# The indexer's keys and 176 of retention's value columns in natural form in the first product

## The chip, the cores and the metric

The kernel runs on one core of one Trainium2 chip. The time is the device time of one execution in microseconds; the time before is the median of three runs, 1668.37 us (1668.28 to 1669.16).

## The reference

One layer of a streaming encoder block on 512 tokens of 2048 channels, all in float32. The normalised input goes through one projection, whose output is cut into the operands of two mixers and two gates. What matters here:

```python
h = rmsnorm(x, norm_gain)
proj = h @ w_in
(aq, ak, av, az, iq, ik, iw, rq, rk, rv, rz, ga, gb) = jnp.split(proj, SPLIT_POINTS, axis=-1)
iq = iq.reshape(B, L, IDX_HEADS, IDX_DIM) * (IDX_DIM ** -0.5)   # 16 heads x 64
ik = plain_layernorm(ik)                                        # 64 columns, normalised per token
iw = iw * (IDX_HEADS ** -0.5)                                   # 16 columns
a_out = dsa_mixer(aq, ak, av, iq, ik, iw, positions, rel_bias) * jax.nn.silu(az)
...
rv = rv.reshape(B, L, R_HEADS, R_VAL_DIM)                       # 8 heads x 128 = 1024 columns
b_out = retention_mixer(rq, rk, rv, ret_gn_gain) * jax.nn.silu(rz)
merged = jax.nn.sigmoid(ga) * (a_out @ w_a_out) + jax.nn.sigmoid(gb) * (b_out @ w_b_out)
r = x + merged @ w_o
return r + (p_i @ w_ple) * jax.nn.sigmoid(r @ w_ple_gate)
```

The index scores are `relu(iq . ik)` weighted with `iw` and summed over the 16 heads; each query keeps its 128 best keys by them.

## The kernel before

**Numbers and products.** A float32 product is made of three matmuls of split operands: `high*high`, `high*low`, `low*high`. The input's parts are `hparts[k]` (names `hh` and `hl`, 128 channels by 512 tokens, for the 16 tiles k of the 2048 channels). A weight arrives by DMA as `wraw`; ScalarE (ACT) converts it to the high part `wh` (L153), VectorE (DVE) subtracts to get the low part `wl` (L158). Such a piece of weight is a unit. There are three buffers each of `wh` and `wl`, so `split_to` works at most two units ahead of the one in use, and `load_to` issues the DMAs five units further ahead from SP's queue, into seven buffers (`RAW_BUFS`).

**Two forms.** In the transposed form the weight is the stationary operand and 384 or 512 tokens move through; the result has channels on partitions. In the natural form 128 tokens of `hh` or `hl` are stationary and weight columns move; the result has tokens on partitions, and there are four token tiles.

**The stages that matter here.** (1) The first product, `gemms` over `u_ik`: the 80 columns `ik` and `iw` in the transposed form (`ps_ikw`, all 512 tokens), and the first 384 columns of `iq` as three blocks (`ps_iq`, 384 tokens), for k = 0 to 15. The weight `w_ik` holds 464 columns. Beside it the input is loaded, split (`x_split`) and squared for the norm (`rms_acc`). (2) The other five blocks of `iq`, meanwhile the norm's sum, and `f_keys1`, `f_keys2`, `f_keys3`: the keys are turned to natural form by four transposes on PE (`ps_kn`), normalised, doubled and turned back. (3) `values`: retention's 1024 value columns in natural form, two blocks of 512 (`ps_vn`, L763 to L765), 16 k by four token tiles by three products each. The blocks are scaled by the token's norm on ACT (L772) and stored to `rd`, from which each head of retention loads its 128 columns much later. Meanwhile PE also makes the index scores (`ps_is`), ACT and DVE sum them (`relu`, `isc`), and the tiles of h are prepared for what follows (`x_steps`: `xn_norm`, and the sums and splits in `combos`, names `ha`, `hs`, `t`). (4) `values_pair`: the attention values, in seven products of units of two k (`ps_v...`, L963 to L965).

**The order of the work.** It is written out by hand; nothing is reordered. PE's loops call `step()` after each group of matmuls (three, in the stages above). A step runs what `later` put on that step, then takes one entry of the queue `todo`; an entry `None` is an empty place. If the entry was empty or `todo` is, and the step's number is a multiple of `state["rate"]`, it takes one entry of the background queue `bg`. So the other engines' instructions are issued in program order at a place that is counted in PE's steps; when they run depends on their engine's own queue and on what they wait for. `todo` holds first the splits of the input (66 entries for the 64 steps of the first product), then the norm, the keys and the index scores; `bg` holds the 8 rounds of `x_steps` (six entries each), some empty entries, the rounds of the top-k and the position bias. The rate is 2 during `values` and 5 during `values_pair`.

Of the kernel before, what the change touches and what calls it, by code (L numbers as in the profile page):

```python
# [9 lines left out]
F32 = mybir.dt.float32  # L10
# [7 lines left out]
L = 512  # L18
# [14 lines left out]
PI_CLAMP = 3.1415925  # L33


def block_kernel(tc, xT, pT, posb, posq, w_in, w_v, w_ik, w_a, w_b, w_o, w_ple, w_gate,
                 w_gt, w_pt, fgb, tab, gains, cst, dec, out, out_a, out_b):
    nc = tc.nc
    pe, dve, act, pool, sp = nc.tensor, nc.vector, nc.scalar, nc.gpsimd, nc.sync
# [1 line left out]
    with contextlib.ExitStack() as ctx:  # L41
# [10 lines left out]
        def U(name, dt=F32):  # L52
            return up.tile([128, L], dt, name=name, tag="u")
# [4 lines left out]
        def P(name):  # L58
            return pp.tile([128, L], F32, name=name, tag="p")
# [122 lines left out]
        def step():  # L182
            tick[0] += 1
            while soon and soon[0][0] <= tick[0]:
                heapq.heappop(soon)[2]()
            f = todo.popleft() if todo else None
            if f is not None:
                f()
            elif bg and (tick[0] % state["rate"] == 0 or state["owed"]):
                state["owed"] = state["hold"]  # L190
                if not state["hold"]:
                    bg.popleft()()
# [145 lines left out]


        K8 = (8, 8)  # L340
        col = lambda g, m: w_in[g + m]
        AQ, AK, AZ, IQ, RQ, RK, RZ, GA, GB = 0, 8, 16, 24, 32, 40, 48, 56, 72
        u_ik = block(w_ik, (1,) * 4 + (2,) * 6, 464)
        u_iq = [None] * 3 + [block(col(IQ, m), K8) for m in range(3, 8)]
        u_rv = [block(w_v[i], (2,) * 8, 512) for i in range(2)]
        u_av = block_wide_pair(w_v[2], w_v[3])
        u_r, u_g = [], []
        for h in range(NH):
            u_r.append(block_pair(col(RQ, h), col(RK, h)))
# [19 lines left out]
        ng, fg, gn = g_sb[:, 0:16], g_sb[:, 16:32], g_sb[:, 32:40]  # L369
        xs = []  # L370
        for k in range(KT):
            if k in (1, 2, 3, 4, 5, 7, 9, 11, 13, 15):
                load_to(state["raw"] + 1)
# [67 lines left out]
        x_split(0)  # L441
        split_to(1)
        step()
        x_split(1)
        split_to(2)
        step()
        sp.dma_start(cs, cst)
        sp.dma_start(pos_i, posb)
# [3 lines left out]
        for k in range(2, KT):  # L452
            todo.append(lambda k=k: x_split(k))
            if k == 2:
                todo.extend([None] * 3)
            else:
                todo.extend([None, None if k % 2 else lambda k=k: rms_acc(xs[k // 2 - 2], k // 2 - 2)] + [None] * (k < 6))
        for k in range(6, KT):
            todo.extend([lambda k=k: rms_acc(xs[k], k), None])

        ps_ikw, *ps_iqs = gemms([(u_ik, slice(0, 80), hparts, ALL, "ps_ikw")]
                                 + [(u_ik, slice(a, a + 128), hparts, slice(128, L), "ps_iq") for a in (80, 208, 336)], 2)

        def iq_split(ps):
            ta = U("ta", F32R)
# [16 lines left out]
        def f_rnat():  # L482
# [4 lines left out]
            dve.tensor_scalar(r2w, r2w, 2.0 ** -5, None, op0=OP.mult)  # L487
            R["r2w"] = r2w


        wq = cp.tile([128, NT, 16], F32, name="wq")

        def f_keys1():
            ps = P("ps_kn")
            for t in range(NT):
                pe.transpose(ps[:, 128 * t:128 * t + 80], kraw[:80, tok(t)], ident[:80, :80])
            kn = U("kn")
            kst = S("kst", 24)
            kmv = S("kmv", 8)
            for t in range(NT):  # L500
                c = slice(128 * t, 128 * t + 64)
                dve.tensor_scalar(kn[:, c], ps[:, c], R["nat"][:, t:t + 1], None, op0=OP.mult)
                dve.tensor_scalar(wq[:, t, :], ps[:, 128 * t + 64:128 * t + 80], R["r2w"][:, t:t + 1], None,
                                  op0=OP.mult)
# [95 lines left out]
            R["ct"], R["st"] = ct, st  # L600

        N3 = [None] * 3
        todo.extend(N3 * 2 + [f_sum] + N3 * 3 + [f_rnat] + N3 * 3 + [f_bcast, None, f_keys1] + N3 * 3 + [f_keys2] + N3 * 2 + [f_keys3] + N3 * 2)
        later(80, f_pos)
        later(88, f_table1)
        later(92, f_table2)
# [48 lines left out]
            return load + [lambda: xn_norm(k)] + [lambda i=i: h_step(k, i) for i in range(X_STEPS)]  # L655

        for m in range(3):
            index_tile(m, ix[m])
# [93 lines left out]
        def values(ids, name, each=lambda s: None):  # L752

            pss = [P("ps_vn") for _ in range(NT)]
            seq = ksteps(ids)
            for s, (i, k) in enumerate(seq):
                if k == 0:
                    split_to(i + AHEAD)
                    load_to(i + AHEAD + LOADS)
                h, l = loaded[i]  # L760
                a, b = hparts[s]
                for t in range(NT):
                    pe.matmul(pss[t], a[:, tok(t)], h[:, k], start=(s == 0), stop=False)  # L763
                    pe.matmul(pss[t], a[:, tok(t)], l[:, k], start=False, stop=False)  # L764
                    pe.matmul(pss[t], b[:, tok(t)], h[:, k], start=False, stop=(s == KT - 1))  # L765
                    step()
                each(s)
            return pss

        def normal(ps, name, t, dt=F32):  # L770
            v = U(name, dt)
            act.activation(v, ps, AF.Copy, scale=R["nat"][:, t:t + 1])  # L772
            return v
# [4 lines left out]
        rd = dp.tile([2, NT, 128, L], F32, name="rd")  # L778

        def retention(h):  # L780

            hc = slice(128 * (h % 4), 128 * (h % 4) + 128)
# [3 lines left out]
            later(32, lambda: sp.dma_start(rv.rearrange("p (t c) -> p t c", t=NT),  # L786
                                           rd[h // 4, :, :, hc].rearrange("t p c -> p t c")))
            ct, st = R["ct"], R["st"]
            E = {}

# [105 lines left out]

        for i in range(2):
            for t, ps in enumerate(values(u_rv[i], "rv", x_load if i else lambda s: None)):
                later(3 * t, lambda i=i, t=t, ps=ps: act.dma_start(rd[i, t], normal(ps, "rv", t)))
        state["rate"] = BG_RATES[1]  # L900


# [471 lines left out]
        todo.extend([None] * 4 + [a_rms, None, a_bc])  # L1374
        todo.extend([lambda m=m: (a_out(m), a_out(m + 1)) for m in range(0, 16, 2)])

        pg, pw = P("ps_tg"), [P("ps_tw") for _ in range(2)]
# [41 lines left out]
            (sp, act, sp)[q].dma_start(out_b[:, L * q:L * q + L], o)  # L1419


MF = 12
U_BUFS = 69
BIG_BUFS = 5
# [20 lines left out]
def _layout(x, p, positions, w_in, norm_gain, w_a_out, w_b_out, w_o, ret_gn_gain,  # L1445
# [8 lines left out]
    def chans(v):  # L1454
# [11 lines left out]
    o["w_v"] = np.concatenate([tiles(w[:, a:a + 1024], 512) for a in (7248, 2048)])  # L1466
    o["w_ik"] = np.ascontiguousarray(
        np.concatenate([w[:, 5120:5200], w[:, 4096:4480]], axis=1).reshape(KT, 128, 464).transpose(1, 0, 2))
# [64 lines left out]
```

## Time and profile before

| | |
|---|---|
| median of three runs | 1668.37 us |
| the profiled execution | 1668.73 us, span 1666.9 us |
| PE (matmuls), PEld (weight loads) busy | 99%, 87% of the span |
| DVE, ACT, POOL busy | 75%, 56%, 15% |
| first product | 5.01 to 42.34 us |
| the other `iq` blocks | 42.34 to about 93.5 us |
| `values`, two blocks | about 93.5 to 191.07 us, the second from 147.55 |
| HBM read, written | 300.21 MB, 41.42 MB |

All times below are microseconds from the start of the span. Matmuls are pipelined: the duration of one is longer than the distance to the start of the next, and that distance is what a further matmul costs. "Idle before" an instruction is idle time of its engine, with what ended it in brackets.

### The profile page before, as it was taken

Reading aid. Unit: us, or ns where it says so; the run is one execution under the profiler, and the core shown is the slowest. Engines: PE = TensorE matmul, PEld = TensorE weight load, DVE = VectorE, ACT = ScalarE, POOL = GpSimd, SP = SyncE. Lnnn points to the kernel's source line nnn. Section 1 sums busy time; section 2 is a strip of 40 time slices with the busy share of each in tenths; the row PEclk is TensorE's granted clock in tenths of the full one; section 3 lists DMA queues with packets and bytes.
Section 4 is the critical chain, followed back from the end, with each engine's and each line's share of the span. In section 5 each row is a group of like instructions: output and inputs, shape, how many; then the busy total and the mean of one; then the engine's idle time right before and its main releaser. Section 6 shows DMA issues by size and latency. Waiting matters only on the chain.

```text
span 1666.9 us, 24622 instructions
## 1 busy us (share of the span) xinstructions
PE 1658.6 (99%) x9174; PEld 1443.8 (87%) x9174; DVE 1252.0 (75%) x1907; ACT 936.8 (56%) x1428; POOL 246.4 (15%) x262
## 2 busy tenths in 40 slices
PE   9999999999999999999999999999999999999998
PEld 8988888888888888888888888888888888888897
DVE  7788889888888888777766676777668887864454
ACT  6556545555555555777776665566633544463342
POOL 2000112111111111111431112100000111112221
PEclk9999999999999999999999999999999999999999
DMA  7327989788788788788898888997466788733222
GB/s 304 114 89 238 320 255 263 202 209 219 192 207 215 192 205 218 204 204 240 238 252 222 220 220 214 268 371 271 154 219 190 186 226 218 205 114 102 83 69 101
DMA packets 121559, 343.25 MB, mean 206 GB/s; under 512 B 13728, under 2 KB 21664, under 8 KB 121440
## 3 DMA queue, kind: packets, MB, share of 16 engines
q1 hardware_dynamic: 84640, 229.71, 40.0%
q0 software_dynamic: 25712, 92.03, 29.5%
q10 hardware_dynamic: 11088, 19.95, 3.3%
q8 instruction: 72, 1.18, 0.3%
q14 instruction: 47, 0.39, 0.1%
HBM read 300.21 MB, written 41.42 MB: 205 GB/s over the span
## 4 chain that ended last, share of the span: by engine, by line
PE 96%; DVE 2%; ACT 1%; issue 0%; DMA 0%; DVEq 0%; SPq 0%; ACTq 0%
PE ps_p L286 24%; PE ps_v L286 16%; PE ps_q L286 8%; PE ps_r L286 8%; PE ps_w L217 3%; PE ps_w L218 3%; PE ps_w L216 3%; PE ps_pg L218 3%; PE ps_pg L217 3%; PE ps_pg L216 3%; PE ps_vn L763 2%; PE ps_vn L765 2%; PE ps_vn L764 2%; PE ps_iq L216 1%; PE ps_iq L217 1%; PE ps_iq L218 1%
## 5 line engine op out<-in xcount | busy, mean ns | idle before, releaser
L158 DVE TENSOR_TENSOR wl<-wraw,wh 128x1024 fp32r<-128x1024 f32 (+3 forms) x460 | 557.2, 1225 | 177.4 <-ACT wh L153 169.4
L153 ACT ACTIVATE wh<-wraw 128x1024 fp32r<-128x1024 f32 (+3 forms) x460 | 474.0, 1040 | 229.6 <-DVE wraw L160 115.4
L119 POOL DMA_DIRECT2D wraw<-w_in x120 | 106.5, 956 | 580.2 <-DVE wl L158 358.6
L286 PE MATMUL ps_p<-hs,wh 128*128 128x512 f32 x640 | 161.1, 393 | 0.0
L249 ACT ACTIVATE e<-ps_p 128x512 f32<-128x512 f32 x144 | 85.9, 596 | 111.7 <-PE ps_p L286 110.0
L286 PEld LDWEIGHTS ps_p<-hs,wh 128*128 128x128 f32 x640 | 114.9, 189 | 20.7 <-issue 0.3
L286 PE MATMUL ps_p<-hs,wl 128*128 128x256 f32 x640 | 92.3, 284 | 0.0
L286 PEld LDWEIGHTS ps_p<-hs,wl 128*128 128x128 f32 x640 | 83.2, 192 | 0.5 <-issue 0.4
L286 PE MATMUL ps_q<-ha,wh 128*128 128x512 f32 x320 | 80.7, 393 | 0.0
L286 PE MATMUL ps_v<-ha,wh 128*128 128x512 f32 x320 | 80.1, 392 | 0.0
L695 ACT ACTIVATE mk<-relf,thr 128x512 f16<-128x512 f32 (+3 forms) x128 | 68.3, 555 | 20.1 <-DVE go L986 13.6
L286 PE MATMUL ps_p<-ha,wh 128*128 128x512 f32 x320 | 79.3, 389 | 0.0
L286 PE MATMUL ps_r<-hs,wh 128*128 128x512 f32 x320 | 79.1, 389 | 0.0
L286 PE MATMUL ps_v<-hs,wh 128*128 128x512 f32 x320 | 79.0, 389 | 0.0
L218 PE MATMUL ps_pg<-rh,wl 128*128 128x512 f32 x192 | 74.8, 390 | 0.0
L217 PE MATMUL ps_pg<-rl,wh 128*128 128x512 f32 x192 | 74.7, 389 | 0.0
L216 PE MATMUL ps_pg<-rh,wh 128*128 128x512 f32 x192 | 74.7, 389 | 0.0
L119 POOL DMA_DIRECT2D wraw<-w_o x24 | 20.9, 931 | 348.8 <-DVE wl L158 316.8
L986 DVE TENSOR_TENSOR go<-e_t 128x256 f32<-128x256 f32 x160 | 68.0, 425 | 5.7
L286 PEld LDWEIGHTS ps_p<-ha,wh 128*128 128x128 f32 x320 | 60.0, 188 | 12.7 <-issue 0.3
L286 PEld LDWEIGHTS ps_r<-hs,wh 128*128 128x128 f32 x320 | 60.1, 188 | 12.5
L286 PEld LDWEIGHTS ps_v<-hs,wh 128*128 128x128 f32 x320 | 60.1, 188 | 12.5
(414 smaller groups left out, 3713.2 us busy)
## 6 DMA issues: line engine op xcount, KB each, us to landing
wraw<-w_in SPq DMA_DIRECT2D x170, 512.0 KB, 5.3
wraw<-w_in POOLq DMA_DIRECT2D x120, 512.0 KB, 8.3
wraw<-w_v SPq DMA_DIRECT2D x32, 512.0 KB, 4.7
wraw<-w_o SPq DMA_DIRECT2D x32, 512.0 KB, 4.8
wraw<-w_o POOLq DMA_DIRECT2D x24, 512.0 KB, 6.4
wraw<-w_gate SPq DMA_DIRECT2D x24, 512.0 KB, 3.8
wraw<-w_b SPq DMA_DIRECT2D x16, 512.0 KB, 5.9
wraw<-w_a SPq DMA_DIRECT2D x16, 512.0 KB, 3.8
```

The lines of the kernel that those rows point to most:

```text
L119: pool.dma_start(out=view(raw_tiles[r], nk, cols), in_=src[:, k0:k0 + nk, :], accum_op=OP.add)
L153: act.activation(h, raw, AF.Copy)
L158: dve.tensor_sub(l, raw, h.bitcast(F32))
L216: pe.matmul(o, h[:, k, w], a, start=(s == order[0]), stop=False)
L217: pe.matmul(o, h[:, k, w], b, start=False, stop=False)
L218: pe.matmul(o, l[:, k, w], a, start=False, stop=(s == order[-1]))
L249: act.activation(E[n], src, AF.Copy)
L286: pe.matmul(o[:, c], w[:, k], X[PRODUCTS[n]][k][:, c], start=(n < 4 and first and k == 0), stop=(ended[n] == 16), skip_group_check=True)
L695: act.activation(bias_e[b][:, ln * i:ln * i + ln], relf[:, :ln], AF.Sign, bias=thr[:, q:q + 1])
L763: pe.matmul(pss[t], a[:, tok(t)], h[:, k], start=(s == 0), stop=False)
L764: pe.matmul(pss[t], a[:, tok(t)], l[:, k], start=False, stop=False)
L986: dve.tensor_add(o[:, q], c0, c1)
```

## The change

The weight `w_ik` now has 640 columns a k: the 80 of `ik` and `iw`, 176 value columns of retention, and the 384 of `iq`. The first product makes the first 256 of them (`N0`) in natural form, four token tiles in four banks, and the 384 of `iq` as before, so each k has 12 + 9 matmuls and seven steps. Each k is a unit of its own; the first k is loaded and split in two pieces. The other 848 value columns are made by `values` in two blocks of 424. The keys come out in natural form, so the four transposes in `f_keys1` go; the 176 value columns are copied to SBUF with the keys (`raw_n`), and scaled and stored to `rd` by four entries that stand in places of `todo` that were empty. `rd` has one row of 1024 columns a token. The entries of `todo` during the first product are spread over its 112 steps. `PHASE` shifts the count of steps that the background goes by, and `FILL` gives the background a fourth empty entry.

```diff
-            elif bg and (tick[0] % state["rate"] == 0 or state["owed"]):
+            elif bg and ((tick[0] + PHASE) % state["rate"] == 0 or state["owed"]):
...
-        u_ik = block(w_ik, (1,) * 4 + (2,) * 6, 464)
+        u_ik = block(w_ik[:, :, 0:N0], (1,), N0) + block(w_ik[:, :, N0:640], (1,), 384)
+        u_ik += [len(units) + i for i in range(KT - 1)]
+        units.extend((raw(w_ik, k, 1, 640), None, 1, 640) for k in range(1, KT))
...
-        u_rv = [block(w_v[i], (2,) * 8, 512) for i in range(2)]
-        u_av = block_wide_pair(w_v[2], w_v[3])
+        u_rv = [block(w_r[i], (2,) * 8, RV[2] - RV[1]) for i in range(2)]
+        u_av = block_wide_pair(w_v[0], w_v[1])
...
             if k == 2:
-                todo.extend([None] * 3)
+                todo.extend([None] * 6)
             else:
-                todo.extend([None, None if k % 2 else lambda k=k: rms_acc(xs[k // 2 - 2], k // 2 - 2)] + [None] * (k < 6))
+                todo.extend([None, None if k % 2 else lambda k=k: rms_acc(xs[k // 2 - 2], k // 2 - 2)]
+                            + [None] * (4 if k < 6 else 1))
...
-        ps_ikw, *ps_iqs = gemms([(u_ik, slice(0, 80), hparts, ALL, "ps_ikw")]
-                                 + [(u_ik, slice(a, a + 128), hparts, slice(128, L), "ps_iq") for a in (80, 208, 336)], 2)
+        ps_n, ps_iqs = [P("ps_vn") for _ in range(NT)], [P("ps_iq") for _ in range(3)]
+        for s, i in enumerate(u_ik[1:]):
+            split_to(i + 2)
+            load_to(i + AHEAD + LOADS)
+            (h, l), (a, b) = loaded[i if s else 0], hparts[s]
+            first, last = s == 0, s == KT - 1
+            for t in range(NT):
+                o = ps_n[t][:, 0:N0]
+                pe.matmul(o, a[:, tok(t)], h[:, 0, 0:N0], start=first, stop=False)
+                pe.matmul(o, b[:, tok(t)], h[:, 0, 0:N0], start=False, stop=False)
+                pe.matmul(o, a[:, tok(t)], l[:, 0, 0:N0], start=False, stop=last)
+                step()
+            h, l = loaded[i]
+            for j in range(3):
...
-        kraw = U("kraw")
-        act.activation(kraw[:80, :], ps_ikw[:80, :], AF.Copy)
-        ix = [iq_split(ps) for ps in ps_iqs[0:2]] + [[]]
-        later(12, lambda i=ix[2]: i.extend(iq_split(ps_iqs[2])))
+        raw_n = [U("raw_n").rearrange("p (a c) -> p a c", a=2) for _ in range(2)]
+        ix3 = [[] for _ in range(3)]
+        for t in range(NT):
+            act.activation(raw_n[t // 2][:, t % 2, 0:N0], ps_n[t][:, 0:N0], AF.Copy)
+        for j in range(3):
+            later(10 + 4 * j, lambda j=j: ix3[j].extend(iq_split(ps_iqs[j])))
...
+        def values_keep(src, t, i, at):
+            n = RV[i + 1] - RV[i]
+            v = U("rv")
+            act.activation(v[:, 0:n], src[:, at:at + n], AF.Copy, scale=R["nat"][:, t:t + 1])
+            act.dma_start(rd[t, :, RV[i]:RV[i + 1]], v[:, 0:n])
...
         def f_keys1():
-            ps = P("ps_kn")
-            for t in range(NT):
-                pe.transpose(ps[:, 128 * t:128 * t + 80], kraw[:80, tok(t)], ident[:80, :80])
...
-        todo.extend(N3 * 2 + [f_sum] + N3 * 3 + [f_rnat] + N3 * 3 + [f_bcast, None, f_keys1] + N3 * 3 + [f_keys2] + ...)
+        todo.extend(N3 * 2 + [f_sum] + N3 * 3 + [f_rnat] + N3 * 3 + [f_bcast, None, f_keys1]
+                    + [lambda t=t: values_keep(raw_n[t // 2][:, t % 2], t, 0, 80) for t in range(NT)]
+                    + [None] * 5 + [f_keys2] + ...)
...
-        bg.extend([lambda: None] * 3)
+        bg.extend([lambda: None] * FILL)
...
-                    pe.matmul(pss[t], a[:, tok(t)], h[:, k], start=(s == 0), stop=False)
+                    o = pss[t][:, 0:RV[2] - RV[1]]
+                    pe.matmul(o, a[:, tok(t)], h[:, k], start=(s == 0), stop=False)
...
+RV = (0, 176, 600, 1024)
+PHASE = -49
+FILL = 4
```

Beside this the input's loads at the start alternate with `w_ik`'s for the first seven k, one step is added ahead of the product, and an empty entry is added to `todo` near the end of the kernel.

More of the change, by code (lines that the diff above doesn't have):

```diff
@@ L33, with block_kernel @@
 PI_CLAMP = 3.1415925
-def block_kernel(tc, xT, pT, posb, posq, w_in, w_v, w_ik, w_a, w_b, w_o, w_ple, w_gate,
+def block_kernel(tc, xT, pT, posb, posq, w_in, w_v, w_r, w_ik, w_a, w_b, w_o, w_ple, w_gate,
                  w_gt, w_pt, fgb, tab, gains, cst, dec, out, out_a, out_b):
@@ L340, in block_kernel @@
         K8 = (8, 8)
+        N0 = 80 + RV[1]
         col = lambda g, m: w_in[g + m]
         AQ, AK, AZ, IQ, RQ, RK, RZ, GA, GB = 0, 8, 16, 24, 32, 40, 48, 56, 72
-        u_ik = block(w_ik, (1,) * 4 + (2,) * 6, 464)
+        u_ik = block(w_ik[:, :, 0:N0], (1,), N0) + block(w_ik[:, :, N0:640], (1,), 384)
+        u_ik += [len(units) + i for i in range(KT - 1)]
+        units.extend((raw(w_ik, k, 1, 640), None, 1, 640) for k in range(1, KT))
         u_iq = [None] * 3 + [block(col(IQ, m), K8) for m in range(3, 8)]
-        u_rv = [block(w_v[i], (2,) * 8, 512) for i in range(2)]
-        u_av = block_wide_pair(w_v[2], w_v[3])
+        u_rv = [block(w_r[i], (2,) * 8, RV[2] - RV[1]) for i in range(2)]
+        u_av = block_wide_pair(w_v[0], w_v[1])
         u_r, u_g = [], []
@@ L371, in block_kernel @@
         for k in range(KT):
-            if k in (1, 2, 3, 4, 5, 7, 9, 11, 13, 15):
-                load_to(state["raw"] + 1)
+            if 0 < k <= RAW_BUFS:
+                load_to(k + 1)
             if k < 10:
@@ L443, in block_kernel @@
         step()
+        split_to(2)
+        step()
         x_split(1)
-        split_to(2)
+        split_to(3)
         step()
@@ L454, in block_kernel @@
             if k == 2:
-                todo.extend([None] * 3)
+                todo.extend([None] * 6)
             else:
-                todo.extend([None, None if k % 2 else lambda k=k: rms_acc(xs[k // 2 - 2], k // 2 - 2)] + [None] * (k < 6))
+                todo.extend([None, None if k % 2 else lambda k=k: rms_acc(xs[k // 2 - 2], k // 2 - 2)]
+                            + [None] * (4 if k < 6 else 1))
         for k in range(6, KT):
             todo.extend([lambda k=k: rms_acc(xs[k], k), None])
-        ps_ikw, *ps_iqs = gemms([(u_ik, slice(0, 80), hparts, ALL, "ps_ikw")]
-                                 + [(u_ik, slice(a, a + 128), hparts, slice(128, L), "ps_iq") for a in (80, 208, 336)], 2)
+        ps_n, ps_iqs = [P("ps_vn") for _ in range(NT)], [P("ps_iq") for _ in range(3)]
[9 more added lines that the diff above has]
+                pe.matmul(o, a[:, tok(t)], l[:, 0, 0:N0], start=False, stop=last)
+                step()
+            h, l = loaded[i]
+            for j in range(3):
+                n = (N0 if s else 0) + 128 * j
+                o, c, w = ps_iqs[j][:, 128:], slice(128, L), slice(n, n + 128)
+                pe.matmul(o, h[:, 0, w], a[:, c], start=first, stop=False)
+                pe.matmul(o, h[:, 0, w], b[:, c], start=False, stop=False)
+                pe.matmul(o, l[:, 0, w], a[:, c], start=False, stop=last)
+                step()
         def iq_split(ps):
@@ L488, in f_rnat @@
             R["r2w"] = r2w
+        rd = dp.tile([NT, 128, 1024], F32, name="rd")
+        def values_keep(src, t, i, at):
[3 more added lines that the diff above has]
+            act.dma_start(rd[t, :, RV[i]:RV[i + 1]], v[:, 0:n])
         wq = cp.tile([128, NT, 16], F32, name="wq")
         def f_keys1():
-            ps = P("ps_kn")
-            for t in range(NT):
-                pe.transpose(ps[:, 128 * t:128 * t + 80], kraw[:80, tok(t)], ident[:80, :80])
             kn = U("kn")
@@ L501, in f_keys1 @@
                 c = slice(128 * t, 128 * t + 64)
-                dve.tensor_scalar(kn[:, c], ps[:, c], R["nat"][:, t:t + 1], None, op0=OP.mult)
-                dve.tensor_scalar(wq[:, t, :], ps[:, 128 * t + 64:128 * t + 80], R["r2w"][:, t:t + 1], None,
-                                  op0=OP.mult)
+                ps = raw_n[t // 2][:, t % 2]
+                dve.tensor_scalar(kn[:, c], ps[:, 0:64], R["nat"][:, t:t + 1], None, op0=OP.mult)
+                dve.tensor_scalar(wq[:, t, :], ps[:, 64:80], R["r2w"][:, t:t + 1], None, op0=OP.mult)
                 dve.bn_stats(kst[:, 6 * t:6 * t + 6], kn[:, c])
@@ L602, in block_kernel @@
         N3 = [None] * 3
-        todo.extend(N3 * 2 + [f_sum] + N3 * 3 + [f_rnat] + N3 * 3 + [f_bcast, None, f_keys1] + N3 * 3 + [f_keys2] + N3 * 2 + [f_keys3] + N3 * 2)
+        todo.extend(N3 * 2 + [f_sum] + N3 * 3 + [f_rnat] + N3 * 3 + [f_bcast, None, f_keys1] + [lambda t=t: values_keep(raw_n[t // 2][:, t % 2], t, 0, 80) for t in range(NT)] + [None] * 5 + [f_keys2] + N3 * 2 + [f_keys3] + N3 * 2)
         later(80, f_pos)
@@ L657, in block_kernel @@
         for m in range(3):
-            index_tile(m, ix[m])
+            index_tile(m, ix3[m])
         for m in range(3, 8):
@@ L762, in values @@
                 for t in range(NT):
-                    pe.matmul(pss[t], a[:, tok(t)], h[:, k], start=(s == 0), stop=False)
-                    pe.matmul(pss[t], a[:, tok(t)], l[:, k], start=False, stop=False)
-                    pe.matmul(pss[t], b[:, tok(t)], h[:, k], start=False, stop=(s == KT - 1))
+                    o = pss[t][:, 0:RV[2] - RV[1]]
+                    pe.matmul(o, a[:, tok(t)], h[:, k], start=(s == 0), stop=False)
+                    pe.matmul(o, a[:, tok(t)], l[:, k], start=False, stop=False)
+                    pe.matmul(o, b[:, tok(t)], h[:, k], start=False, stop=(s == KT - 1))
                     step()
@@ L768, in values @@
             return pss
[L770 to L773, printed above, removed]
         yd, bd, zd, qd, kd = (dp.tile([NH, 128, L], F32, name=n) for n in ("yd", "bd", "zd", "qd", "kd"))
         vd = dp.tile([2, 7, 128, L], F32, name="vd")
-        rd = dp.tile([2, NT, 128, L], F32, name="rd")
         def retention(h):
-            hc = slice(128 * (h % 4), 128 * (h % 4) + 128)
+            hc = slice(128 * h, 128 * h + 128)
             g128 = (1.0 - 2.0 ** (-5.0 - h)) ** 128
@@ L786, in retention @@
             later(32, lambda: sp.dma_start(rv.rearrange("p (t c) -> p t c", t=NT),
-                                           rd[h // 4, :, :, hc].rearrange("t p c -> p t c")))
+                                           rd[:, :, hc].rearrange("t p c -> p t c")))
             ct, st = R["ct"], R["st"]
@@ L898, in block_kernel @@
             for t, ps in enumerate(values(u_rv[i], "rv", x_load if i else lambda s: None)):
-                later(3 * t, lambda i=i, t=t, ps=ps: act.dma_start(rd[i, t], normal(ps, "rv", t)))
+                later(3 * t, lambda i=i, t=t, ps=ps: values_keep(ps, t, i + 1, 0))
         state["rate"] = BG_RATES[1]
@@ L1372, in a_out @@
                 sp.dma_start(o, t[:, :, A])
-        todo.extend([None] * 4 + [a_rms, None, a_bc])
+        todo.extend([None] * 5 + [a_rms, None, a_bc])
         todo.extend([lambda m=m: (a_out(m), a_out(m + 1)) for m in range(0, 16, 2)])
@@ L1465, in _layout @@
                                 ((0, 2048), (3072, 5120), (5200, 7248), (8272, 13392))])
-    o["w_v"] = np.concatenate([tiles(w[:, a:a + 1024], 512) for a in (7248, 2048)])
-    o["w_ik"] = np.ascontiguousarray(
-        np.concatenate([w[:, 5120:5200], w[:, 4096:4480]], axis=1).reshape(KT, 128, 464).transpose(1, 0, 2))
+    o["w_v"] = tiles(w[:, 2048:3072], 512)
+    o["w_r"] = tiles(w[:, 7248 + RV[1]:7248 + 1024], RV[2] - RV[1])
+    o["w_ik"] = tiles(np.concatenate([w[:, 5120:5200], w[:, 7248:7248 + RV[1]], w[:, 4096:4480]], axis=1), 640)[0]
     o["w_a"] = tiles(np.asarray(w_a_out)[0])
```

## Prediction

> **What bounds the kernel now.** I read the page first, for the shares and for the chain that ended last.
>
> ```profile
> span 1666.9 us, 24622 instructions
> ...
> PE 1658.6 (99%) x9174; PEld 1443.8 (87%) x9174; DVE 1252.0 (75%) x1907; ACT 936.8 (56%) x1428; POOL 246.4 (15%) x262
> ...
> PE 96%; DVE 2%; ACT 1%; issue 0%; DMA 0%; DVEq 0%; SPq 0%; ACTq 0%
> ```
>
> PE is busy 99% of the span and makes up 96% of the chain. A busy PE could still be a waiting one, so the list of waits came next, for PE alone; its longest line is this one:
>
> ```profile
> PE ps_warm L410 <- DVE warm L388: 1.0, 1, 1.0
> ```
>
> That is before the first matmul. So in the whole run PE hardly waits for anybody: the time is the number of matmuls times the distance from one start to the next. An edit is worth its change in PE time, and nothing more, as long as no other engine starts to hold PE up. Both have to be worked out for this change. The work around it is issued from PE's steps, so what matters of the other engines is how near they are to PE in the stages whose matmuls are moved. I therefore took the timeline for the distances, and then the busy time of each engine by stage.
>
> **The matmuls of the first product.** The timeline of PE, two rounds of k and the start of the next stage:
>
> ```profile
> 8.30 0.39 PE L216 MATMUL ps_ikw<-hh,wh 128*80 128x512 f32 x1
> ...
> 37.81 0.39 PE L216 MATMUL ps_ikw<-hh,wh 128*80 128x512 f32 x1
> ...
> 38.50 0.34 PE L216 MATMUL ps_iq<-hh,wh 128*128 128x384 f32 x1
> ...
> 40.07 0.39 PE L216 MATMUL ps_ikw<-hh,wh 128*80 128x512 f32 x1
> ...
> 42.34 0.33 PE L216 MATMUL ps_iq<-hh,wh 128*128 128x384 f32 x1
> ```
>
> One k is three matmuls for the 80 key columns (0.69 us from 37.81 to 38.50) and nine for the queries (1.57 us to 40.07). The second k starts at 8.30 and the next stage at 42.34, so 15 rounds take 34.04 us, 2.269 us each. After the change the three become twelve of 256 columns (four token tiles, three products). The kernel has that width elsewhere, with a new stationary tile for each matmul as here, in runs of eight:
>
> ```profile
> 505.83 1.11 PE L286 MATMUL ps_q<-ha,wl 128*128 128x256 f32 x8
> 506.79 1.12 PE L286 MATMUL ps_r<-hs,wl 128*128 128x256 f32 x8
> ```
>
> 0.96 us for eight is 0.120 us each. Twelve are 1.44 us, with the nine unchanged 3.01 us, so a round grows by 0.741 us and sixteen by 11.9 us. The first round has a start-up loss of its own: it runs from 5.01 to 8.30, 3.29 us instead of 2.27. Its first load is smaller now (256 columns instead of 464), its second comes separately. I take the loss of 1.02 us as unchanged and keep both ends: it can vanish or double, one microsecond either way.
>
> **The matmuls of the two value blocks.** The stretches of busy time, of which the second last is exactly the second block (16 k, four tiles, three products: 192 matmuls):
>
> ```profile
> 5.01:42.34 37.33, 37.33 (x194) 33.23 (x193) 31.38 (x33) 27.08 (x43) 11.19 (x7) 1.00 0.81 316
> 42.34:60.00 17.66, 17.66 (x109) 17.66 (x109) 12.09 (x18) 9.35 (x14) 1.02 (x1) 1.00 0.43 129
> 123.75:147.55 23.80, 23.80 (x110) 19.80 (x108) 21.33 (x45) 13.41 (x26) 0.00 (x0) 1.00 0.54 180
> 147.55:191.07 43.52, 43.52 (x194) 36.04 (x192) 39.78 (x84) 26.44 (x55) 4.86 (x6) 1.00 0.98 315
> 93.50:191.07 97.57, 97.57 (x445) 81.33 (x443) 87.11 (x182) 56.45 (x111) 4.86 (x6) 1.00 0.64 207
> ```
>
> The columns are the stretch, its length, then the busy time of PE, PEld, DVE, ACT and POOL, the clock, the DMA share and GB/s. 43.52 us over 192 is 0.2267 us for 512 columns. Against 0.120 us for 256 that is 0.417 ns a column. 88 columns less are 0.0367 us a matmul, and 384 matmuls give back 14.1 us.
>
> The Trainium skill, "TensorE: Matmul & The Clock Gate", section "Back-to-back issue gap", gives the gap as the columns over 2.4 GHz plus about 2.5 ns. By that rule the first product would grow by 10.6 us instead of 11.9, as an estimate; the value blocks would still give back 14.1. The rows differ from it: 0.2267 and 0.120 us lie some 11 ns above its 215.8 and 109.2 ns, and twelve short matmuls carry that rest more often than three long ones.
>
> **The transposes.** The key transposes on PE go; their group, and the matmul behind it:
>
> ```profile
> 60.27 0.44 PE L496 MATMUL ps_kn<-cs,kraw 80*128 80x80 f32 x4
> 60.50 0.42 PE L216 MATMUL ps_iq<-hh,wh 128*128 128x384 f32 x1
> ```
>
> They held PE for 0.23 us, and I count 0.3 with the slower pair behind them. PE's sum is 11.9 - 14.1 - 0.3 = -2.5 us.
>
> **What is added beside PE.** ScalarE gets four copies of 256 columns at the end of the first product, in place of one of 512, then four scalings of 176 columns with four stores; the eviction of the later blocks is shorter by 88 columns. SP issues seven loads more (17 instead of 10 for the first product).
>
> ```profile
> L249 ACT ACTIVATE e<-ps_p 128x512 f32<-128x512 f32 x144 | 85.9, 596 | 111.7 <-PE ps_p L286 110.0
> 190.94 0.33 ACTq L899 DMA_DIRECT2D rd<-rv  x1
> 15.01 0.33 SPq L132 DMA_DIRECT2D wraw<-w_ik  x1
> ```
>
> Eight evictions at no more than 0.596 us and four issues of 0.33 are under 6.1 us, where ACT works 9.35 us of the 17.66 behind the product: covered, and PE's next weights there are split two units ahead. If that cover failed, PE would wait for what exceeds the 8.3 us of idle, nothing here. The seven SP issues, 2.3 us, fall in a product that becomes 49 us long; behind them stand only later loads. In the product itself DVE works 31.38 us of 37.33 and gets sixteen rounds of 176 more columns to split; with 0.19 us for each (below) that is 34.4 of 49 us, so it is looser than before.
>
> **Where DVE meets PE.** In the value stage the reverse holds. DVE is busy 87.11 us of 97.57. What it does there (splits, index sums, the steps that prepare the 16 tiles of h for the next stage) is issued from PE's steps and only the splits shrink. The price of a split:
>
> ```profile
> L158 DVE TENSOR_TENSOR wl<-wraw,wh 128x1024 fp32r<-128x1024 f32 x14 | 17.1, 1224 | 3.6 <-ACT wh L153 3.3
> L158 DVE TENSOR_TENSOR wl<-wraw,wh 128x928 fp32r<-128x928 f32 x6 | 6.7, 1120 | 1.4 <-ACT wh L153 1.3
> ```
>
> 96 columns are 0.104 us, so 176 are 0.19. Fourteen splits give 2.7 us: 84.4 us of DVE work in 97.57 - 14.1 = 83.5 us. That doesn't fit, even without any idle. How late it gets, and for whom, the timeline of DVE and PE shows:
>
> ```profile
> 123.75 0.75 DVE L628 SCALAR_TENSOR_TENSOR isc<-relu,wq,isc 128x512 f32<-128x512 f32 x1 [0.59 <-ACT relu L621]
> ...
> 189.21 1.22 DVE L158 TENSOR_TENSOR wl<-wt,wh 128x1024 fp32r<-128x1024 f32 x1
> 190.35 1.09 DVE L304 TENSOR_TENSOR hs<-t,hs 128x256 fp32r<-128x256 f32 x3
> ...
> 193.79 0.39 PE L963 MATMUL ps_vv<-wh,hs 128*128 128x512 f32 x1
> 194.01 0.39 PE L964 MATMUL ps_vv<-wl,hs 128*128 128x512 f32 x1
> ```
>
> At 123.75 DVE last waited for something that PE had to bring first (a score, through ACT). From there on its idle comes from ACT, not from PE. The low half of the attention values' second unit is done at 190.43 and PE reads it at 194.01: 3.58 us to spare, with PE's stage of attention values starting at 191.07.
>
> After the change PE covers that stretch sooner by 288 matmuls (192 and half the first block) times 0.0367, 10.6 us. DVE saves ten splits, 1.9 us. The queue of steps helps: the old first product has 64 steps for 66 entries, and two entries spill into the next stage; the new one has 112 steps for 88. So everything behind runs two steps (2 x 0.57 us) earlier against PE, 1.1 us; PHASE sets the count of ticks right (48 steps of the product and one before it), and FILL's added empty entry returns the top-k rounds to their old tick. That same shift puts one entry of the preparation more ahead of the split in question, two subtractions, about 0.7 us by the row of three in 1.09. The spare time becomes 3.58 - 10.6 + 1.9 + 1.1 - 0.7 = -4.7 us, plus what DVE wins back of its idle: 67.32 us less 61.11 busy, 6.2 us in the two stretches up to 191.07. Most of that is ACT and DVE handing halves to each other, which stays; some is ACT's conversion and eviction, which shrink. I take 1.3 of the 6.2, so a stall of 3.4 us, between 0 and 4.7. Behind it the background slows from every second to every fifth step, so DVE catches up.
>
> The sum is -2.5 + 3.4 = +0.9 us. The profiled execution took 1668.73 us, its span of 1666.9 and 1.8 around it, 0.4 above the median of 1668.37; put on the median, the forecast is 1669.3 us. What this measurement can tell from no change is about 0.2%, 3.3 us.
>
> **The rivals.** *DVE keeps up.* ACT and DVE pack closer, PE never waits, and the sum of the matmuls stands alone: 1668.37 - 2.5 = 1665.9 us. For it: the 6.2 us of idle exceed the missing 4.7. Against it: ACT is idle too in that stretch, so the idle is a chain of hand-overs, not lack of work. With the start-up loss gone as well it would be 1664.9.
>
> *PE goes cold.* The stall is one gap at one unit, and it decides whether the clock falls back. What a cold PE costs shows at the start:
>
> ```profile
> 0.99 4.45 PE L410 MATMUL ps_warm<-warm 128*128 128x512 bf16 x10 [0.99 <-DVE warm L388]
> ...
> 6.52 0.52 PE L216 MATMUL ps_iq<-hh,wh 128*128 128x384 f32 x1
> 6.84 0.38 PE L217 MATMUL ps_iq<-hl,wh 128*128 128x384 f32 x1
> ```
>
> At 6.52 a matmul of 384 columns still takes 0.32 us to the next, later 0.174. From 0.99 to 6.84 PE is slow, 5.85 us, in which it does what takes 3.2 us warm: 2.7 us lost. With the stall that gives 1669.3 + 2.7 = 1672.0 us, slower than before. It decides from a gap without matmuls about as long as my largest single one. The clock row of this trace shows no drop after the start, and no gap to test it on. The Trainium skill, "TensorE: Matmul & The Clock Gate", section "HAM oscillation — how this bites in real kernels", puts the border at idle gaps above about 3.4 us; no run here shows it yet.
>
> *Loads are late.* The DMA share is 0.98 in the second block at 315 GB/s. If that is a ceiling, the 43.52 us of transfers don't fit in 43.52 - 7.0 = 36.5 us, and the loads of the attention values come up to 7.0 us later: up to +4.5 us, 1672.9. Against it: the first product moves as much at a share of 0.81, and these loads are issued several units ahead.
>
> **How the numbers follow.** The forecast case (a stall of 1 to 4.7 us) gets 0.55, DVE keeping up 0.25, the cold clock 0.15, late loads 0.05. Faster by over 0.2% means below 1665.0: only the first rival with a better start reaches it, 0.10. Slower by over 0.2% means above 1671.7: most of the cold clock and of the late loads, 0.18. Within it stays 0.72. The range takes the first rival with its start-up gain nearly whole and goes to the late loads' end: 1665.0 to 1672.9. The likeliest case alone spans 1666.9 to 1670.6.
>
> **What would show it.** Right: twelve matmuls of 256 columns at 0.120 us and a round of 3.0 us in the first product; 0.190 us for 424 columns; DVE over 95% busy in the value stage; the first waits of PE in the run, on the low halves, within 6 us of the start of the attention values, summing to 1 to 4.7 us. Wrong: no PE wait there (then the first rival), a clock below full behind the gap (the second), ACT waiting for the values' weights there (the third), or rounds of the first product away from 3.0 us, which would break the sum itself.

## The result and the profile after

The changed kernel takes 1671.41 us (median of 16 runs, 1669.31 to 1676.21) against 1668.34 us before (16 runs, 1668.23 to 1669.88). The ratio is 1.0018, 95% interval 1.001 to 1.0025: about 3 us slower, where 1669.3 us was forecast, with a range to 1672.9. New is the spread: 7 us instead of 1.7. The profiled execution is the slowest of the 16 (1676.21 us, span 1674.4), so its waits are read here for their kind; their usual size comes from a second trace below.

The page's totals, and the list of waits for PE alone (in total, times, longest):

```profile
span 1674.4 us, 24961 instructions
...
PE 90%; DVE 4%; DMA 3%; ACT 2%; issue 1%; ACTq 0%; DVEq 0%; SPq 0%
```

```profile
PE ps_vp L991 <- ACT wh L153: 3.8, 1, 3.8
PE ps_warm L413 <- DVE warm L391: 1.0, 1, 1.0
PE ps_vv L991 <- ACT wh L153: 0.9, 1, 0.9
PE ps_vv L992 <- DVE wl L158: 0.8, 1, 0.8
PE ps_vp L992 <- DVE wl L158: 0.6, 1, 0.6
```

Before there was hardly a wait of PE; now there are four at the attention values, 6.1 us together. The timeline of PE says what the matmuls did, and where the waits lie:

```profile
4.98 0.38 PE L477 MATMUL ps_vn<-wh,hh 128*128 128x256 f32 x1 [0.24 <-ACT wh L153]
...
8.66 0.28 PE L477 MATMUL ps_vn<-wh,hh 128*128 128x256 f32 x1
...
50.84 0.28 PE L477 MATMUL ps_vn<-wh,hh 128*128 128x256 f32 x1
...
188.25 0.35 PE L799 MATMUL ps_vn<-wh,hl 128*128 128x424 f32 x1
188.44 0.39 PE L991 MATMUL ps_vv<-wh,hs 128*128 128x512 f32 x1
...
190.94 0.39 PE L993 MATMUL ps_vv<-wh,hs 128*128 128x512 f32 x1
192.23 0.51 PE L991 MATMUL ps_vv<-wh,hs 128*128 128x512 f32 x1 [0.90 <-ACT wh L153]
193.49 0.51 PE L992 MATMUL ps_vv<-wl,hs 128*128 128x512 f32 x1 [0.76 <-DVE wl L158]
...
204.28 0.39 PE L993 MATMUL ps_vp<-wh,ha 128*128 128x512 f32 x1
208.52 0.67 PE L991 MATMUL ps_vp<-wh,ha 128*128 128x512 f32 x1 [3.85 <-ACT wh L153]
209.78 0.80 PE L992 MATMUL ps_vp<-wl,ha 128*128 128x512 f32 x1 [0.59 <-DVE wl L158]
210.37 0.63 PE L993 MATMUL ps_vp<-wh,ha 128*128 128x512 f32 x1
210.80 0.63 PE L991 MATMUL ps_vp<-wh,ha 128*128 128x512 f32 x1
```

Rounds of the first product: 14 from 8.66 to 50.84, 3.013 us each. 424 columns: 0.19 us to the next start. The attention values begin at 188.44 instead of 191.07: 2.63 us sooner. Then come two gaps of 1.06 and 1.03 us (a start less the start before it and the 0.23 us that a matmul of 512 columns takes), for the second unit's high half from ACT and low half from DVE; the clock stays at 1.00 there. At 204.28 follow two more, 4.0 and 1.0 us, and behind them a matmul takes 0.43 us instead of 0.227. The stretches of busy time (PE, PEld, DVE, ACT, POOL, then the clock, DMA share, GB/s):

```profile
105.30:188.44 83.14, 83.14 (x442) 80.89 (x440) 78.27 (x169) 49.22 (x102) 4.57 (x5) 1.00 0.63 192
123.75:140.00 16.25, 16.25 (x89) 15.69 (x88) 16.08 (x32) 10.10 (x19) 0.00 (x0) 1.00 0.31 92
204.28:215.50 11.22, 6.78 (x17) 4.65 (x16) 5.67 (x9) 4.54 (x6) 0.00 (x0) 0.70 1.05 340
```

DVE is busy 94% of the value stage and 99% of a part of it, and the clock behind the long gap is down to 0.70 in the mean of its stretch. Where that long gap comes from, ACT's timeline shows:

```profile
199.06 0.60 ACT L523 ACTIVATE rv<-ps_vn,r_nat 128x424 f32<-128x424 f32 x1
206.96 0.33 ACTq L524 DMA_DIRECT2D rd<-rv  x1
207.41 1.06 ACT L153 ACTIVATE wh<-wraw 128x1024 fp32r<-128x1024 f32 x1 [7.76 <-DMA wraw<-w_v]
```

The last store of the value block, ready at 199.66, is issued at 206.96; only then can ACT convert the next weight. The landing of a weight load released it, and the chain of the run has the same hand-over. It is that load, issued by SP at 187.18, which landed at 206.88:

```profile
187.18 19.70 DMA wraw<-w_v
206.88 0.02 issue
206.91 0.02 ACTq L524
```

In this kernel the 650 loads and stores of SP and ACT use eight semaphores (the counters by which a landing is told), 81 or 82 times each, and in the whole trace each of them is issued only after the one before it on its semaphore has landed. The store at 206.96 and the load at 187.18 share one. The load's landing is told in sixteen increments; fifteen of them come by 201.69, the last at 206.88. With such a load a store can stand at the head of ACT's queue.

### The profile page after: what moved, and what is told of

Same layout as the page of the kernel before. It is cut to its first block, busy times and chain, and to the rows that moved or that the text cites. A ratio compares the mean times of both kernels' runs of the same rounds, so it can differ in the third digit from the quotient of the medians.

```text
span 1674.4 us, 24961 instructions
## 1 busy us (share of the span) xinstructions
PE 1659.5 (99%) x9314; PEld 1460.1 (87%) x9314; DVE 1252.3 (75%) x1914; ACT 939.4 (56%) x1442; POOL 246.5 (15%) x262
## 4 chain that ended last, share of the span: by engine, by line
PE 90%; DVE 4%; DMA 3%; ACT 2%; issue 1%; ACTq 0%; DVEq 0%; SPq 0%
PE ps_p L286 24%; PE ps_v L286 16%; PE ps_q L286 8%; PE ps_r L286 8%; PE ps_w L217 3%; PE ps_w L216 3%; PE ps_w L218 3%; PE ps_pg L218 3%; PE ps_pg L217 3%; PE ps_pg L216 3%; DMA wraw<-w_v 1%; PE ps_iq L216 1%; PE ps_iq L218 1%; PE ps_iq L217 1%; DMA xn<-xT 1%
## 5 line engine op out<-in xcount | busy, mean ns | idle before, releaser
L158 DVE TENSOR_TENSOR wl<-wraw,wh 128x1024 fp32r<-128x1024 f32 (+4 forms) x467 | 561.7, 1216 | 189.4 <-ACT wh L153 183.3
L153 ACT ACTIVATE wh<-wraw 128x1024 fp32r<-128x1024 f32 (+4 forms) x467 | 475.4, 1028 | 240.4 <-DVE wraw L160 120.9
L728 ACT ACTIVATE mk<-relf,thr 128x512 f16<-128x512 f32 (+3 forms) x128 | 68.3, 555 | 20.4 <-DVE go L1014 13.6
```

The costliest lines, as they stand in the source:

```text
L153: act.activation(h, raw, AF.Copy)
L158: dve.tensor_sub(l, raw, h.bitcast(F32))
L728: act.activation(bias_e[b][:, ln * i:ln * i + ln], relf[:, :ln], AF.Sign, bias=thr[:, q:q + 1])
```

## The experiments

**The changed kernel again.** No edit.

> The changed kernel once more, for a second trace beside the slow one of 1676.2 us. Theory: PE's matmuls are 2.6 us shorter up to the start of the attention values; behind it PE waits about 2 us for DVE's low halves of the second unit, in every execution; what differs between executions (1669.3 to 1676.2 us) is a further wait, because a store of the second value block stands at the head of ACT's queue until the lane of DMA that it shares with a weight load is free. Median 1671 us, ratio 1.001 to 1.003. Rival: the wait on DVE is what varies, from 1 to 7 us, and no store holds ACT up.

1672.02 us (10 runs, 1669.31 to 1673.77; ratio 1.0018, 1.0009 to 1.0027); the profiled execution took 1672.83. Timeline of PE and stretches:

```profile
193.90 0.80 PE L991 MATMUL ps_vv<-wh,hs 128*128 128x512 f32 x1 [2.47 <-ACT wh L153]
195.16 0.80 PE L992 MATMUL ps_vv<-wl,hs 128*128 128x512 f32 x1 [0.46 <-DVE wl L158]
195.75 0.63 PE L993 MATMUL ps_vv<-wh,hs 128*128 128x512 f32 x1
```

```profile
188.53:193.50 4.97, 2.90 (x13) 2.07 (x12) 3.68 (x10) 2.18 (x5) 0.00 (x0) 1.00 1.06 335
193.50:200.50 7.00, 6.13 (x14) 4.47 (x15) 5.14 (x10) 4.83 (x9) 1.80 (x3) 0.51 1.04 360
```

Here the second unit's wait is 2.63 + 1.03 us, 3.7 together, no store holds ACT up, and the clock is at half for 6.8 us, from 193.70 on: it falls 0.2 us before the first of the two matmuls. Set against the kernel before, matmul by matmul, PE is 2.5 us ahead at the start of the attention values, 1.2 behind after the two gaps and 3.8 behind when the clock is back: 2.6 us for the slow clock. The theory that a store makes the usual excess fails on this trace.

What made the high half late stands on the timelines of DVE and ACT, first of this run, then of DVE in the kernel before:

```profile
189.60 0.75 DVE L682 SCALAR_TENSOR_TENSOR xn<-xn,g_sb,r_b 128x512 f32<-128x512 f32 x1 [1.97 <-DMA xn<-xT]
...
192.81 1.04 ACT L153 ACTIVATE wh<-wt 128x1024 fp32r<-128x1024 f32 x1
```

```profile
184.99 1.41 DVE L649 SCALAR_TENSOR_TENSOR xn<-xn,g_sb,r_b 128x512 f32<-128x512 f32 x2
```

DVE stood still for 1.97 us because the load of x for the last tile of h had not landed, and ACT converts the second unit only behind that tile's sums and splits. The load was issued at 175.1, 13.4 us ahead of the attention values, and took 14.4 us. In the kernel before it was issued 22.7 us ahead of them, took 11.0 us and had landed 6 us before DVE used it. DVE's idle time for this load is 0.29 us in the first trace and 1.43 to 1.97 us in the three others in which the tiles of h are prepared in the order of the change (this one, the late stores, the filled wait).

**Stores of the second block 48 steps later.**

```diff
-            act.dma_start(rd[t, :, RV[i]:RV[i + 1]], v[:, 0:n])
+            later(lag, lambda: act.dma_start(rd[t, :, RV[i]:RV[i + 1]], v[:, 0:n]))
...
-  values_keep(ps, t, i + 1, 0)
+  values_keep(ps, t, i + 1, 0, 48 * i)
```

> The four stores of the second value block are issued 48 steps later, behind the crowded stretch; nothing else differs. Theory of the store: ACT no longer stands still ahead of the sixth unit's conversion, PE's wait there (4.0 and 1.0 us in the trace) goes and with it the slow clock behind it; the wait on DVE at the second unit (2.2 us) stays. 1668.0 to 1669.0 us, with a narrow spread. Rival, the loads themselves are late: the wait stays about as long, on the weights of that unit, and the time stays at 1671.

1671.53 us (11 runs, 1670.17 to 1674.84; ratio 1.0019, 1.001 to 1.0028): no gain, the theory of the store was wrong as to the median. PE's waits:

```profile
PE ps_vv L991 <- ACT wh L153: 2.2, 1, 2.2
PE ps_warm L413 <- DVE warm L391: 1.0, 1, 1.0
PE ps_vv L992 <- DVE wl L158: 0.8, 1, 0.8
```

```profile
195.40:198.80 3.40, 3.40 (x10) 2.62 (x9) 3.01 (x4) 2.32 (x4) 1.66 (x2) 0.51 1.05 419
```

The sixth unit's wait is not there, the second unit's is (gaps of 2.3 and 1.0 us), and the clock is at half for 3.4 us behind it. DVE's idle time for the load of x is 1.62 us here.

**The first pair of tiles of h prepared early.** Its five entries stand in empty places of `todo` among the keys; the empty entries of the background go from 4 to 10, so that the top-k keeps its step. The first pair's load of x is issued earlier, and with it every later pair's by one round.

```diff
-  ... + [None] * 5 + [f_keys2] + N3 * 2 + [f_keys3] + N3 * 2)
+  ... + [None, lambda: xn_norm(0), None, lambda: h_step(0, 0), None, f_keys2, None, lambda: h_step(0, 1), None,
+         lambda: h_step(0, 2), None, lambda: h_step(0, 3), f_keys3] + N3 * 2)
...
+        later(16, lambda: xn_load(0))
...
-        bg.append(lambda: xn_load(0))
-        for k in range(8):
+        bg.append(lambda: xn_load(1))
+        for k in range(1, 8):
...
-FILL = 4
+FILL = 10
```

> The preparation of the first pair of tiles of h (two norms, the sums and splits, 5 to 6 us of DVE) stands in empty places of the keys' stretch, ahead of the index scores, so the other seven pairs come about 7 us sooner against PE; the top-k stays at its step. Theory of DVE: the low half of the second unit of the attention values is done before PE asks for it, and the wait of 2.2 us there goes; the store's wait may stay. 1669 to 1670 us. Rival, DVE is late for another reason (the loads of x, or ACT): the wait at the second unit stays above 1.5 us.

1668.52 us (11 runs, 1668.18 to 1669.67; ratio 1.0, 0.9991 to 1.0009). Of the waits at the second unit 0.2 us is left:

```profile
PE ps_warm L413 <- DVE warm L391: 1.0, 1, 1.0
PE ps_is L654 <- DVE ikl L562: 0.6, 1, 0.6
PE ps_vn L479 <- DVE wl L158: 0.4, 1, 0.4
PE ps_vv L995 <- DVE wl L158: 0.2, 1, 0.2
```

This run alone does not say why. There are 5 to 6 us less of DVE's work behind the keys, but the last load of x also lands 3.4 us before DVE uses it, and PE comes to the attention values 2.4 us later than in the first trace, which by itself hides most of a wait. The place had a price: the turning of the keys and the first score came later, and PE was only 0.27 us ahead at the attention values.

**Both edits.**

> Both edits. Theory: PE waits for nobody in the value stages, and the sum of the matmuls alone stands: 1668.4 - 2.6 = 1665.8 us, from 1665.5 to 1666.5, a ratio of 0.998 to 0.999. Rival: one wait gives way to the next (late loads), and less than 3 us of the 5.6 come back.

1669.02 us (11 runs, 1668.32 to 1671.4; ratio 1.0004, 0.9995 to 1.0012). The late stores add nothing, and the expected 1665.8 us missed the price of the early place.

**The narrow value blocks alone.** The kernel before, with blocks of 424 columns; 176 value columns are left out.

```diff
-        u_rv = [block(w_v[i], (2,) * 8, 512) for i in range(2)]
+        u_rv = [block(w_r[i], (2,) * 8, 424) for i in range(2)]
...
-                    pe.matmul(pss[t], a[:, tok(t)], h[:, k], start=(s == 0), stop=False)
+                    pe.matmul(pss[t][:, 0:424], a[:, tok(t)], h[:, k], start=(s == 0), stop=False)
```

> The kernel before with one part of the change alone: its two value blocks are 424 columns wide, the first product is the old one with the keys transposed. 176 value columns are left out. Theory: the narrow blocks take 14 us off PE, and the same two waits appear at the attention values, since DVE's work and the stores are as dense as in the changed kernel: 2 to 7 us come back, 1656 to 1661 us. Rival, the longer first product or its loads make the waits: no wait, 1654.2 us.

1659.05 us (4 runs, 1658.07 to 1659.3; ratio 0.9941, 0.9924 to 0.9957). The attention values begin at 177.49, 13.6 us sooner, but the time is only 9.3 us shorter: 4.2 us of that come back, and PE waits at the same place:

```profile
180.01 0.39 PE L967 MATMUL ps_vv<-wh,hs 128*128 128x512 f32 x1
182.10 0.49 PE L965 MATMUL ps_vv<-wh,hs 128*128 128x512 f32 x1 [1.71 <-ACT wh L153]
183.43 0.50 PE L966 MATMUL ps_vv<-wl,hs 128*128 128x512 f32 x1 [0.83 <-DVE wl L158]
```

```profile
183.90:187.30 3.40, 3.40 (x10) 2.61 (x9) 2.04 (x4) 2.61 (x4) 1.10 (x2) 0.50 1.02 351
```

The shorter value stage is enough to make the wait, without the longer first product and its loads. DVE does not wait for a load of x here, so the work of DVE and ACT is enough, too. Behind gaps of 1.86 and 1.10 us the clock is at half for 3.4 us.

**Both edits in the kernel before.**

> The kernel before with the two edits of the last experiment (first pair of tiles prepared early, stores of the second block 48 steps later). Theory: PE waited for nobody there, so nothing comes back: 1668.0 to 1668.8 us. Rival, the two edits are worth something by themselves, and the gain of the last experiment is not the removal of the change's waits: 1 us or more faster.

1672.73 us (10 runs, 1671.22 to 1673.99; ratio 1.0024, 1.0015 to 1.0033): a miss. Nothing was won, but 4 us were lost. In its trace PE waits 1.1 us for DVE at the turned keys (`ps_kT`) and is 2.0 us behind at the attention values; the rest that the median lost is not placed by this trace, whose own execution took 1671.52.

**The first pair early, spread behind the keys.** The entries stand behind `f_keys3` and in the empty places ahead of the third and fourth block of index scores; the loads of x and the empty entries are as in the first early run, the first load 8 steps later.

```diff
-  ... + [f_keys3] + N3 * 2)
+  ... + [f_keys3] + [None, lambda: xn_norm(0), None, None, lambda: h_step(0, 0), None])
...
+        X0 = {2: [lambda: h_step(0, 1), None, lambda: h_step(0, 2)], 3: [None, lambda: h_step(0, 3), None]}
...
-                todo.extend(N3)
+                todo.extend(X0.get(m, N3))
```

> The first pair of tiles of h is prepared early again, but behind the turning of the keys and between the first index scores, so that the keys are not held up (the earlier place cost 2.3 us before the attention values). Theory of DVE: PE reaches the attention values about 2.5 us sooner than in the kernel before, does not wait there by more than 0.5 us, and the clock stays full: 1665.8 to 1666.8 us, ratio 0.9983 to 0.9992. Rival, one wait gives way to the next (the loads of the attention values): a wait of 1 us or more elsewhere in that stage, and 1667.5 us or more.

1666.76 us (11 runs, 1666.43 to 1667.25; ratio 0.999, 0.9981 to 0.9999): faster than both kernels, with a spread of 0.8 us. PE's waits, and the stretches about the start of the attention values at 188.66:

```profile
PE ps_warm L413 <- DVE warm L391: 1.0, 1, 1.0
PE ps_vn L477 <- ACT wh L153: 0.3, 1, 0.3
PE ps_r L286 <- ACT wh L153: 0.2, 1, 0.2
```

```profile
188.66:193.50 4.84, 4.84 (x23) 4.01 (x22) 2.58 (x3) 3.12 (x4) 2.37 (x3) 1.00 1.04 390
193.50:200.50 7.00, 7.00 (x33) 5.79 (x32) 5.90 (x12) 3.97 (x6) 0.89 (x1) 1.00 1.07 287
```

PE is busy throughout at full clock, though the DMA share is as high as in the changed kernel. PE comes to the attention values as early as in the change, and no wait is left there: the wait does not go merely because PE comes late. Less work of DVE and ACT and the earlier loads of x are still not told apart: the last load lands 2.7 us before its use. PE is 2.4 us ahead at the attention values, 1.7 at the end; no run explains the 0.7 between.

**The wait filled.** Sixteen matmuls of zeros ahead of the second unit.

```diff
+                    if n == 0 and s == 2:
+                        for _ in range(16):
+                            pe.matmul(banks[b][0].rearrange("p (a c) -> p a c", a=4), zer,
+                                      zer[:, None, :].to_broadcast([128, 4, 128]), start=False, stop=False, ...)
```

> The changed kernel with sixteen matmuls of zeros (512 columns, bfloat16) added ahead of the second unit of the attention values, where PE waits 2 to 4 us; they add nothing to the sums and take about 3.5 us. Theory of the cold clock: the wait itself is only filled, but the clock does not drop behind it, so the 1.7 to 3.4 us that a drop costs go: about 1669.5 us, within 1669.0 to 1670.0, with a narrow spread and no dip of the clock. Rival, the dip has nothing to do with the gap: it stays, and with the fill the time is 1671.5 us or more.

1670.15 us (11 runs; ten from 1669.48 to 1671.74, one at 1676.05; ratio 1.0014, 1.0006 to 1.0023). Timeline and clock of the profiled execution (1669.48 us):

```profile
191.15 3.63 PE L992 MATMUL ps_vv<-zer 128*128 128x512 bf16 x16
194.43 0.58 PE L998 MATMUL ps_vv<-wh,hs 128*128 128x512 f32 x1
194.84 0.39 PE L999 MATMUL ps_vv<-wl,hs 128*128 128x512 f32 x1
```

```profile
193.50:200.50 7.00, 7.00 (x32) 5.40 (x31) 5.16 (x9) 5.33 (x9) 2.41 (x3) 1.00 1.04 354
```

PE loses 3.3 us there, as long as in the waits before, but it works on zeros meanwhile, and the clock stays at 1.00 where it was 0.51. Eight of the eleven runs have a mean clock of 0.999 over the span, against three of the sixteen of the change. The median is 1.3 us below the changed kernel's, although the fill takes its 3.3 us whether PE would have waited or not: the slow clock follows from the gap. The run at 1676.05 shows that something rarer is left; no trace has caught it.

**The spread early pair in the kernel before.**

> The kernel before with the early preparation of the first pair of tiles alone, spread as in the run with the changed kernel. Theory: PE waited for nobody in the kernel before, so there is nothing to win: 1668.1 to 1668.9 us. Rival: the early place is worth something by itself, 1 us or more faster.

1669.03 us (10 runs, 1668.81 to 1671.62; ratio 1.0006, 0.9997 to 1.0015). Slightly above what was expected and no gain: the early place is worth something only with the change.

## Why the prediction was right, and where it was off

**PE's sum.** Forecast -2.5 us, measured -2.63 (and -2.53 in the second trace). A round came to 3.013 us against 3.01, 424 columns to 0.19 us. The start-up loss shrank a little: the first round takes 3.68 us, 0.39 more than before instead of 0.74.

**The wait on DVE.** Forecast 3.4 us, between 0 and 4.7, at the second unit of the attention values. Measured 2.1 us in the first trace, 3.7 and 3.3 in the next two of such kernels, 3.0 with the narrow blocks alone. The place was right; the size is right in part by luck. In those three traces 0.29, 1.97 and 1.62 us of DVE's idle time wait for the load of x, which the sum did not have. What is left, as an estimate, is 1.8, 1.7 and 1.7 us for the work of DVE and ACT, half of the 3.4: if the sum's other terms hold, some 3 us of DVE's 6.2 us of idle time came back, not 1.3. Two details differ: the longer part of the wait is for the high half from ACT, which stands behind the same hand-overs, the shorter for DVE's subtraction; and DVE is 94% busy in the value stage, not over 95%.

**The cold clock.** This is the step that was wrong. It was made a rival with a chance of 0.15 because the border was put at a gap about as long as the largest single one; it is the more frequent case. Three traces have it at the second unit: with a single gap of 2.63 us (the clock fell at its end, ahead of the second gap), and with gaps of 2.3 + 1.0 and 1.86 + 1.10 us with one matmul between the two; only 1.06 + 1.03 us passed without it. In the 3.4 us ahead of the three drops PE was idle for 2.4, 2.8 and 2.7 us; in 3.4 us around the two gaps without a drop, for 2.1 at most.

The rival's price of 2.7 us compares with 2.6 for a drop of 6.8 us and some 1.7 for one of 3.4, and its sum, 1672.0, is close to the median. The 16 runs of the changed kernel agree: the three at a mean clock of 0.999 took 1669.3 to 1670.1 us, the eight at 0.998 took 1670.1 to 1671.9, the five at 0.996 or 0.997 took 1672.1 to 1676.2. 3.4 us at half the clock lose 1.7 us, a thousandth of the span. These clocks are rounded to a thousandth, and one profiled run without a drop also shows 0.998 (the spread early pair), so they say that drops are frequent, not in which of the eight runs. So the likeliest case should have been wait and drop together, about +2.6 to +3.5 us instead of +0.9; the median moved by +3.1. The likeliest case spans 1666.9 to 1670.6, and 1671.4 lies above it. That the stated range holds it is owed to the rivals at its upper end.

The Trainium skill, "TensorE: Matmul & The Clock Gate", section "HAM oscillation — how this bites in real kernels", sets the border at idle gaps above about 3.4 us. The runs differ: 1.86 us and 1.10 us with a matmul between were enough. By the same page of the Trainium skill, section 'Part 1: The HAM clock gate (the "warmup" mystery)', the watching window is 3.4 us long and runs freely; the drops last 3.4 or 6.8 us here, one or two such windows.

**Late loads.** This rival had a chance of 0.05 and meant the weights of the attention values. What was late in four traces is the load of x for the last tile of h, which held DVE up for 0.3 to 2.0 us and, through it, ACT's conversion of the second unit. In the first trace a weight load that took 19.7 us to land also held PE up, for 5 us and a drop of the clock, but through a store on ACT's queue and not as the weight that PE needed. That store is not the median's cause: later stores changed nothing there. How often it strikes is open.

**DVE keeps up.** In none of the 26 runs of the change (the fastest took 1669.3 us); the kernel with the spread early pair is what that rival described, at 1666.8 us against its 1665.9.

## What to carry to other kernels

When PE never waits, a change that shortens PE's work in one stage is worth only what every engine whose work is issued from that stage's steps can follow. Compare their busy time with the new length of the stage first, and the time that loads have to land; move the work that no longer fits, and its loads, to an earlier place. In these traces waits of 3.0 to 3.7 us cost another 1.7 to 2.6 us in clock, and one of 2.1 us cost none.

## What the runs showed of the hardware that was not expected

After two gaps of 1.86 and 1.10 us, with one matmul between, PE's clock was at half for 3.4 us; after two of 1.06 and 1.03 us it was not. Sixteen matmuls of zeros in the gap kept the clock at 1.00. And a store of 212 KB stood 7.3 us at the head of ACT's queue, because the last of the sixteen increments of the transfer before it on its semaphore had not come.
